# Two trunk layers on one core: features in four loads, an early activation, first products of one feature tile, and other numbers for the planner

## Chip, core and metric

The kernel runs on one core of a Trainium2 chip. The metric is the device time of one execution in microseconds (us), lower is better. Before the change three runs took 1011.51, 1011.09 and 1009.39 us; the median is 1011.09 us.

## What is computed

The reference is a two-layer backbone that serves 128 context tokens and 256 latent tokens with the same weights. Cut to what matters here, one layer is:

```python
m = silu(cvec) @ w_mod + b_mod                     # six vectors of 1024: shift, scale, gate, twice
h = rms(x, g_mix) * (1 + scale) + shift            # "modulated" features
cq, ckv, krope, na_q, na_k, na_v, df_q, df_k, df_v = split(h @ w_in)
o_mla, o_na, o_df = attention_A(...), attention_B(...), attention_C(...)
x = x + gate * (concat(o_mla, o_na, o_df) @ w_out)
h = rms(x, g_ffn) * (1 + scale2) + shift2
x = x + gate2 * ((silu(h @ w_gate) * (h @ w_up)) @ w_down)
```

All weights are float32. A float32 product is made as three matmuls of split halves: high x high, high x low, low x high (helper `mm3`, L357 to L359).

## The kernel before, in words

The features lie transposed in one tile `xT`, eight feature tiles (`KD = 8`) of 128 rows by 384 tokens. A layer has a planned part and a part in fixed order. The planned part holds everything from the modulation to the first output tiles: each step is a task with an engine, an assumed duration, the tasks it waits for, the buffers it takes, and a priority. The class `Plan` lays these tasks out in time with the assumed durations, tries 300 random changes of the priorities, and keeps the order that ends first in its own model. That order is then what each engine executes, strictly in sequence. So a changed duration in the plan can move any task of either layer. The FFN behind it has a fixed order.

The start of layer 0, where the changed lines stand, goes like this:

- **Loads.** SyncE issues `xT` in two halves (L260), then, in the plan's order, the modulation weights (`qu`, `ku` and `raw` from `w_mod`, L398) and the input weights (`raw` from `w_in`, L312). The small vector `cv` comes on ScalarE's queue.
- **Fillers.** TensorE begins with matmuls of `ones` with `ones` (L750) that compute nothing needed. Two numbers give how many (`WARMUP`): 18 at once and 16 pairs, which the plan may put wherever TensorE has nothing to do. One filler is two instructions in the profile.
- **Statistics.** ScalarE applies SiLU to `cv` (`sv`, L743), then squares the eight feature tiles (L759); VectorE adds them up (L763); TensorE sums over partitions (`t`, L771); GpSimd takes the power -1/2 (L522), VectorE makes a diagonal (L527), TensorE spreads it (L531), ScalarE copies it out (`bc`, L739).
- **Modulation.** Shift and scale come in four sets, each serving two feature tiles. A set is two steps of 16 matmuls (`m`, L408), one for each half of its weights, then a copy (L414), a transpose (L419), and the bias and scale on VectorE (L425, L454).
- **Modulated features.** For each feature tile: multiply by the norm (`nt`, L546), scale and shift (L554, on VectorE or GpSimd as `POOLK` says), high half (`hh`, ScalarE, L550), low half (`hl`, VectorE, L558).
- **First products.** The column chunks 0 and 1 of `w_in` are split into halves (`wh` on ScalarE, L285; `wl` on VectorE, L291) and multiplied with `hh` and `hl` for three token tiles each. A unit of the plan takes two feature tiles: six matmuls. With three token tiles, two chunks and four pairs this makes 24 units or, counted by single feature tiles, 48.

The attention of the layer follows, with more of `w_in` as dense work between its small matmuls.

## Time and profile before

| | before |
|---|---|
| median of three runs | 1011.09 us |
| the profiled execution | 1011.29 us |
| its span on the core | 1009.5 us |
| TensorE matmul busy | 995.5 us (99%) |
| VectorE busy | 721.8 us (71%) |
| ScalarE busy | 512.6 us (51%) |
| GpSimd busy | 174.4 us (17%) |
| first product (L357) starts | 22.87 us after the span's start |

Times of instructions are microseconds from the span's start. The busy share of TensorE includes the fillers and the overlap of pipelined matmuls, so a share of 99% doesn't say that 99% of the time is needed work. A row of the timeline gives start, length, engine, line, operation and tile; what stands in brackets is the idle time of that engine before it and what ended it. PE is TensorE's matmul, PEld its weight load, SPq SyncE's queue of DMA issues.

### The profile page before, as it was taken

How to read it: one execution, taken by the hardware profiler on the slowest of the kernel's cores; microseconds unless marked ns; L12 is line 12 of the kernel's file. 1: busy time of each engine (PE TensorE's matmuls, PEld its weight loads, DVE VectorE, ACT ScalarE, POOL GpSimd, SP SyncE). 2: the span in 40 equal slices, each digit the busy share in tenths (PEclk: the TensorE clock that was granted, in tenths of full speed). 3: DMA queues.
4: the chain of work that ended last, by engine and by line, in shares of the span. 5: the costliest groups of instructions: out<-in, count | busy, mean ns of one | idle time of the engine just before them, and what ended most of it. 6: DMA issues, size and time to landing. Idle time of an engine off the chain costs nothing.

```text
span 1009.5 us, 16623 instructions
## 1 busy us (share of the span) xinstructions
PE 995.5 (99%) x6074; PEld 929.6 (92%) x6074; DVE 721.8 (71%) x1637; ACT 512.6 (51%) x1206; POOL 174.4 (17%) x263
## 2 busy tenths in 40 slices
PE   9999999999999999999999999999999999999998
PEld 8877778899999999999978878888999999999998
DVE  4678778887999999964356887788889655554342
ACT  3466778765433333333326778796553433333221
POOL 2166123201000000100015633240010000000000
PEclk9999999999999999999999999999999999999999
DMA  9865643327575757684462143322574525244451
GB/s 361 329 200 180 193 135 125 108 87 255 186 242 186 240 181 225 188 278 136 126 216 96 48 152 90 106 89 82 195 243 148 165 88 163 85 127 123 131 146 37
DMA packets 128209, 163.82 MB, mean 162 GB/s; under 512 B 5120, under 2 KB 107136, under 8 KB 125824
## 3 DMA queue, kind: packets, MB, share of 16 engines
q1 hardware_dynamic: 119712, 134.33, 41.5%
q0 software_dynamic: 6832, 27.77, 7.9%
q8 instruction: 48, 0.79, 0.3%
q10 hardware_dynamic: 1584, 0.66, 0.2%
q14 instruction: 33, 0.27, 0.1%
HBM read 159.69 MB, written 3.05 MB: 161 GB/s over the span
## 4 chain that ended last, share of the span: by engine, by line
PE 89%; ACT 5%; DVE 2%; POOL 1%; DMA 1%; issue 1%; ACTq 0%; DVEq 0%; POOLq 0%
PE z L357 13%; PE z L359 13%; PE z L358 13%; PE t L358 6%; PE t L357 6%; PE t L359 6%; PE s L357 5%; PE s L358 5%; PE s L359 5%; PE s L1078 4%; PE t L1045 2%; PE m L408 2%; PE t L1181 1%; PE s L952 1%; PE s L750 1%
## 5 line engine op out<-in xcount | busy, mean ns | idle before, releaser
L285 ACT ACTIVATE wh<-raw 128x768 fp32r<-128x768 f32 (+3 forms) x224 | 203.5, 909 | 365.4 <-PE z L358 138.1
L291 DVE TENSOR_TENSOR wl<-raw,wh 128x768 fp32r<-128x768 f32 (+3 forms) x224 | 231.8, 1035 | 112.5 <-ACT wh L285 110.9
L357 PE MATMUL z<-fh,wh 128*128 128x386 f32 x304 | 103.2, 339 | 0.0
L358 PE MATMUL z<-fl,wh 128*128 128x386 f32 x304 | 103.1, 339 | 0.0
L357 PE MATMUL z<-wh,hh 128*128 128x384 f32 (+1 forms) x264 | 101.3, 384 | 1.8 <-ACT hh L550 1.4
L359 PE MATMUL z<-fh,wl 128*128 128x386 f32 x304 | 102.6, 338 | 0.0
L480 DVE CUSTOM_DVE_ANT_0 sums<-wt,sums,pcol 128x1024 f32<-128x1024 f32 x80 | 102.3, 1278 | 0.3 <-ACT sums L469 0.3
L359 PE MATMUL z<-wh,hl 128*128 128x384 f32 (+1 forms) x264 | 90.5, 343 | 0.5 <-DVE hl L558 0.5
L358 PE MATMUL z<-wl,hh 128*128 128x384 f32 (+1 forms) x264 | 90.0, 341 | 0.0
L578 POOL TENSOR_TENSOR small<-small,mhalf 128x4 f32<-128x4 f32 (+4 forms) x58 | 75.5, 1302 | 4.8
L357 PE MATMUL s<-fh,wh 128*128 128x386 f32 x200 | 68.2, 341 | 0.0
L357 PE MATMUL t<-fh,wh 128*128 128x386 f32 x200 | 68.1, 340 | 0.0
L358 PE MATMUL t<-fl,wh 128*128 128x386 f32 x200 | 67.8, 339 | 0.0
L358 PE MATMUL s<-fl,wh 128*128 128x386 f32 x200 | 67.7, 339 | 0.0
L359 PE MATMUL s<-fh,wl 128*128 128x386 f32 x200 | 67.5, 338 | 0.0
L359 PE MATMUL t<-fh,wl 128*128 128x386 f32 x200 | 67.5, 338 | 0.0
L1101 ACT ACTIVATE e<-s,small 128x384 f32<-128x384 f32 (+1 forms) x114 | 57.8, 513 | 15.2 <-DVE small L1090 9.0
L474 POOL DMA_DIRECT2D wt<-in_w_modT x40 | 21.5, 539 | 252.4 <-DVE mod L480 186.5
L357 PEld LDWEIGHTS z<-wh,hh 128*128 128x128 f32 x264 | 50.0, 189 | 11.0 <-issue 4.6
L358 PEld LDWEIGHTS z<-fl,wh 128*128 128x128 f32 x304 | 57.5, 189 | 0.0
L359 PEld LDWEIGHTS z<-fh,wl 128*128 128x128 f32 x304 | 57.3, 189 | 0.0
L357 PEld LDWEIGHTS z<-fh,wh 128*128 128x128 f32 x304 | 57.2, 188 | 0.0
(299 smaller groups left out, 2414.4 us busy)
## 6 DMA issues: line engine op xcount, KB each, us to landing
raw<-in_w_gate SPq DMA_DIRECT2D x22, 1024.0 KB, 6.2
raw<-in_w_up SPq DMA_DIRECT2D x22, 1024.0 KB, 5.4
raw<-in_w_down SPq DMA_DIRECT2D x32, 704.0 KB, 4.7
wt<-in_w_modT POOLq DMA_DIRECT2D x40, 512.0 KB, 4.1
raw<-in_w_mod SPq DMA_DIRECT2D x16, 1024.0 KB, 5.1
raw<-in_w_in SPq DMA_DIRECT2D x40, 384.0 KB, 4.0
raw<-in_w_out SPq DMA_DIRECT2D x8, 640.0 KB, 4.4
qu<-in_w_mod SPq DMA_DIRECT2D x8, 512.0 KB, 8.5
```

What stands on the lines that cost most here:

```text
L285: nc.scalar.activation(hi, src, AF.Copy)
L291: nc.vector.tensor_tensor(lo, src, hi.bitcast(F32), op=ALU.subtract)
L357: nc.tensor.matmul(out, sh, mh, start=first, stop=False)
L358: nc.tensor.matmul(out, sh, ml, start=False, stop=False)
L359: nc.tensor.matmul(out, sl, mh, start=False, stop=last)
L408: nc.tensor.matmul(self.pm[32 * g:32 * g + 32, :n], sv[:, kb + k, :], w[g // self.per][:, k, i * n:(i + 1) * n], start=(kb + k == 0), stop ...
L474: nc.gpsimd.dma_start(self.w[:, self.loaded % 3], w_modT[l, c * P:(c + 1) * P])
L480: nc.vector.tensor_tensor_reduce(self.junk, self.w[:, self.n % 3], self.s[:, v], 1.0, pcol[l][:, PC_BMOD + c:PC_BMOD + c + 1], ALU.mult, A ...
L578: nc.gpsimd.tensor_tensor(out, t[:, :n], mhalf[:, :n], op=ALU.pow)
L1045: nc.tensor.transpose(pt[:, b, :], x, ident)
L1078: nc.tensor.matmul(ps[:, i, :], q, k, start=True, stop=True)
L1101: nc.scalar.activation(x["e"][i], ps[:, j, :], AF.Exp, bias=x["mx"][:, i:i + 1], scale=-1.0 if bias else 1.0, accum_out=x["su"][:, i:i + 1])
```

## The change

- `xT` is loaded in four pieces of two feature tiles instead of two pieces of four; the squares wait for their own piece.
- An activation with SiLU on one column of `ones` is put right behind the issue of `cv`; its result is overwritten with the old constant.
- For the chunks 0 and 1 of layer 0 a unit of the first products takes one feature tile: three matmuls.
- The fillers become 24 at once and 40 single ones.
- One feature tile of layer 0 (tile 1) moves from GpSimd to VectorE for its scale and shift.
- The plan's assumed numbers change: the lag of a DMA 2.8 to 2.0, a modulation load 2.95 to 2.62, the first loads, the scale and shift 1.08/0.6 to 1.36/0.64. The lag and the last two hold for both layers.

The diff, cut to its core:

```diff
-POOLK = ((1, 3, 5, 7), (0, 2, 3, 4, 5, 6, 7))
+POOLK = ((3, 5, 7), (0, 2, 3, 4, 5, 6, 7))
-LAG = 2.8
+LAG = 2.0
-WARMUP = (18, 0.43, 16)
+WARMUP = (24, 0.215, 40)
-LOADX = 2.6
+LOADX = (2.3, 0.98)
...
     nc.scalar.dma_start(cv, cv_d)
+
+    nc.scalar.activation(mhalf[:, 15:16], ones[:, 0:1], AF.Silu)
+    nc.vector.memset(mhalf[:, 15:16], -0.5)
...
-    for k in range(0, KD, 4):
-        nc.sync.dma_start(xT[:, k:k + 4, :], xT_d[:, k:k + 4, :])
+    for k in range(0, KD, 2):
+        nc.sync.dma_start(xT[:, k:k + 2, :], xT_d[:, k:k + 2, :])
...
-            w = w0 = add(PE, WARMUP[1] / 2 * WARMUP[0], lambda *a: idle(WARMUP[0], *a), take=("s",), prio=URGENT)
+            w = w0 = add(PE, WARMUP[1] * WARMUP[0], lambda *a: idle(WARMUP[0], *a), take=("s",), prio=URGENT)
             for i in range(WARMUP[2]):
-                w = add(PE, WARMUP[1], lambda: idle(2), after=[w], prio=DENSE + 9)
+                w = add(PE, WARMUP[1], lambda: idle(1), after=[w], prio=DENSE + 9)
             add(DVE, 0.0, lambda: None, after=[w], frees=[w0])
-            sums, loaded = [], [add(DMA, LOADX, lambda: None, prio=0.0) for _ in range(2)]
+            add(DMA, LOADX[0], lambda: None, prio=4 * URGENT)
+            sums, loaded = [], [add(DMA, LOADX[1], lambda: None, prio=2 * URGENT) for i in range(4)]
...
-                sums.append(add(ACT, 0.42, square, after=[loaded[k // 4]], take=("row",), prio=k))
+                sums.append(add(ACT, 0.42, square, after=[loaded[k // 2]], take=("row",), prio=k))
...
-                    ld = add(DMA, 2.95, lambda *kind, ms=ms, kb=kb: ms.load(kb, *kind), take=("un|raw",), prio=PPRIO[part])
+                    ld = add(DMA, 2.62, lambda *kind, ms=ms, kb=kb: ms.load(kb, *kind), take=("un|raw",), prio=PPRIO[part])
...
-            b = add(POOL if on_pool else DVE, 1.08 if on_pool else 0.6, lambda k=k, x=x, e=nc.gpsimd if on_pool else nc.vector: norm_aff(l, k, x["t"], e),
+            b = add(POOL if on_pool else DVE, 1.36 if on_pool else 0.64, lambda k=k, x=x, e=nc.gpsimd if on_pool else nc.vector: norm_aff(l, k, x["t"], e),
...
-                    u = add(PE, 6 * (n / 2400 + 0.0135), unit, after=[lo, last[t], hready[kb], hready[kb + 1]],
-                            take=((kind[t] if len(kind) > 1 else kind),) if kb == 0 else (), frees=[hi], prio=DENSE)
+                    for k in ((0,), (1,)) if l == 0 and ci < 2 else ((0, 1),):
+                        def unit(*tag, t=t, kb=kb, w=w, ks=k):
...
+                        u = add(PE, 3 * len(k) * (n / 2400 + 0.0135), unit, after=[lo, last[t]] + [hready[kb + i] for i in k],
+                                take=((kind[t] if len(kind) > 1 else kind),) if first else (), frees=[hi], prio=DENSE)
```

What the plan makes of it stands in the order of the instructions. The changed file is longer, so a line of before has a number that is 3 lower at this place (L750 is L753 after). First TensorE, from the kernel's start to its first product, before: `s` is the fillers' bank, `t` the sum and the spread of the statistics and the transpose, `m` a modulation set, whose two halves of weights are told apart by the number of `qu`, and `z` the first product. Rows that only repeat are left out.

```order
L750 MATMUL s_137<-ones 128x128 x34
L408 MATMUL m_206<-qu_157,sv 32x128 x2
L771 MATMUL t_223<-ones,sq_163 128x1 x3
L750 MATMUL s_137<-ones 128x128 x6
L408 MATMUL m_206<-qu_176,sv 32x128 x2
L531 MATMUL t_265<-dg_259,ones 128x384
L750 MATMUL s_137<-ones 128x128 x4
L419 MATMUL t_283<-ident,mev_269 128x128
L750 MATMUL s_137<-ones 128x128 x6
L408 MATMUL m_303<-qu_235,sv 32x128 x2
L408 MATMUL m_303<-qu_275,sv 32x128 x2
L357 MATMUL z_359<-wh_263,hh_119 128x416
```

The same stretch after the change, and the first step of the second set (`m_351`) behind the first product.

```order
L753 MATMUL s_141<-ones 128x128 x26
L775 MATMUL t_200<-ones,sq_169 128x1 x3
L411 MATMUL m_204<-qu_171,sv 32x128 x2
L753 MATMUL s_141<-ones 128x128 x6
L534 MATMUL t_239<-dg_231,ones 128x384
L753 MATMUL s_141<-ones 128x128 x9
L411 MATMUL m_204<-qu_221,sv 32x128 x2
L753 MATMUL s_141<-ones 128x128 x6
L422 MATMUL t_302<-ident,mev_289 128x128
L753 MATMUL s_141<-ones 128x128 x17
L360 MATMUL z_339<-wh_284,hh_123 128x416
L411 MATMUL m_351<-qu_298,sv 32x128 x2
```

Four steps of `m` stand ahead of the first product before, two after; 50 fillers become 64, and of those behind the sum of the squares 16 become 38. The second half of the first set now stands behind the spread and nine fillers; it stood ahead of the spread.

SyncE's loads at the start, before (`qu_157` and `qu_176` with their `ku` are the two halves of the first modulation set, `qu_235` begins the second):

```order
L260 DMA xT<-in_xT 128x1536 x2
L398 DMA qu_157<-in_w_mod 128x1024
L398 DMA ku_158<-in_w_mod 128x1024
L398 DMA qu_176<-in_w_mod 128x1024
L398 DMA ku_177<-in_w_mod 128x1024
L312 DMA raw_204<-in_w_in 128x832
L312 DMA raw_227<-in_w_in 128x768
L398 DMA qu_235<-in_w_mod 128x1024
```

And after. Here `qu_171` and `qu_221` are the halves of the first set; `qu_192` and `ku_193` between them belong to the third set, whose matmuls come behind the second's.

```order
L263 DMA xT<-in_xT 128x768 x4
L401 DMA qu_171<-in_w_mod 128x1024
L401 DMA ku_172<-in_w_mod 128x1024
L401 DMA qu_192<-in_w_mod 128x1024
L401 DMA ku_193<-in_w_mod 128x1024
L401 DMA qu_221<-in_w_mod 128x1024
L401 DMA ku_222<-in_w_mod 128x1024
L315 DMA raw_241<-in_w_in 128x832
L315 DMA raw_249<-in_w_in 128x768
L401 DMA qu_261<-in_w_mod 128x1024
```

The second half of the first set has moved two transfers of 512 KB back.

VectorE from the first set's scale to the first low halves, before:

```order
L454 SCALAR_TENSOR_TENSOR aff_103<-mod_101,pcol_105 128x4
L554 TENSOR_SCALAR nt_287<-nt_287,aff_103,mod_101 128x256
L554 TENSOR_SCALAR nt_287<-nt_287,aff_103,mod_101 128x128
L291 TENSOR_TENSOR wl_300<-raw_227,wh_281 128x768
L558 TENSOR_TENSOR hl_120<-nt_287,hh_119 128x384
```

And after, where the scale and shift of the second feature tile (`nt_259`) stands on VectorE too, ahead of the first low half:

```order
L457 SCALAR_TENSOR_TENSOR aff_107<-mod_105,pcol_109 128x4
L557 TENSOR_SCALAR nt_251<-nt_251,aff_107,mod_105 128x256
L557 TENSOR_SCALAR nt_251<-nt_251,aff_107,mod_105 128x128
L557 TENSOR_SCALAR nt_259<-nt_259,aff_107,mod_105 128x256
L557 TENSOR_SCALAR nt_259<-nt_259,aff_107,mod_105 128x128
L294 TENSOR_TENSOR wl_324<-raw_249,wh_295 128x768
L561 TENSOR_TENSOR hl_124<-nt_251,hh_123 128x384
```

Behind the start the plans of both layers are reshuffled as well. Counted over TensorE's whole order: from the end of the 48 first products to the FFN of layer 0 the dense products (L357 to L359) are resumed after other work 44 times before and 57 times after; in layer 1's planned part 63 times before and 66 after. The rows of the FFN stand as they were, but for the places where they meet the planned part.

More of the change, by code (lines that the diff above doesn't have):

```diff
@@ L819, in weights @@
                 if pairs:
-                    lead = add(DMA, 2.95 / 4096 * n, lambda: w_raw(rk, src, rs, 0), take=("raw", "graw"), prio=pairs[0])
-                    lead.mate = add(DMA, 2.95 / 4096 * n, lambda: w_raw(rk, src, rs, 1), after=[lead], prio=pairs[1])
+                    lead = add(DMA, 2.62 / 4096 * n, lambda: w_raw(rk, src, rs, 0), take=("raw", "graw"), prio=pairs[0])
+                    lead.mate = add(DMA, 2.62 / 4096 * n, lambda: w_raw(rk, src, rs, 1), after=[lead], prio=pairs[1])
                 else:
@@ L840, in g1 @@
                 for t in range(3):
-                    def unit(*tag, t=t, kb=kb, w=w):
-                        if tag:
-                            z[t] = acc(tag[0])
-                        s = slice(t * P, (t + 1) * P)
-                        for k in range(2):
-                            mm3(z[t][:, :n], hh[:, kb + k, s], hl[:, kb + k, s], w["h"][:, k, :], w["l"][:, k, :],
-                                kb + k == 0, kb + k == KD - 1)
-                    u = add(PE, 6 * (n / 2400 + 0.0135), unit, after=[lo, last[t], hready[kb], hready[kb + 1]],
-                            take=((kind[t] if len(kind) > 1 else kind),) if kb == 0 else (), frees=[hi], prio=DENSE)
-                    u.dense = 1
-                    plan.dense += 1
-                    last[t] = u
-                    if kb == 0:
-                        room[t] = u
+                    for k in ((0,), (1,)) if l == 0 and ci < 2 else ((0, 1),):
+                        def unit(*tag, t=t, kb=kb, w=w, ks=k):
+                            if tag:
+                                z[t] = acc(tag[0])
+                            s = slice(t * P, (t + 1) * P)
+                            for k in ks:
+                                mm3(z[t][:, :n], hh[:, kb + k, s], hl[:, kb + k, s], w["h"][:, k, :], w["l"][:, k, :],
+                                    kb + k == 0, kb + k == KD - 1)
+                        first = kb + k[0] == 0
+                        u = add(PE, 3 * len(k) * (n / 2400 + 0.0135), unit, after=[lo, last[t]] + [hready[kb + i] for i in k],
+                                take=((kind[t] if len(kind) > 1 else kind),) if first else (), frees=[hi], prio=DENSE)
+                        u.dense = 1
+                        plan.dense += 1
+                        last[t] = u
+                        if first:
+                            room[t] = u
                     if kb == KD - 2 and done:
```

## The prediction

> **What bounds the kernel now.** I read the page first, then busy time by stage, then the timeline of the first 60 us. The page names TensorE:
>
> ```profile
> span 1009.5 us, 16623 instructions
> PE 995.5 (99%) x6074; PEld 929.6 (92%) x6074; DVE 721.8 (71%) x1637; ACT 512.6 (51%) x1206; POOL 174.4 (17%) x263
> ```
>
> The profiled execution took 1011.29 us, so 1.8 us lie outside its span; it is 0.2 us above the median of 1011.09. All sums below are made against 1011.29. What a measurement here can tell from no change is about 0.2%, that is 2 us.
>
> The stages, with the columns stretch, length, then TensorE's busy time and count first (rows of the stages from the first products on; the last of the three is layer 1's planned part):
>
> ```profile
> 22.87:57.43 34.56, 34.52 (x294) 30.31 (x292) 21.31 (x76) 18.63 (x52) 7.91 (x17) 1.00 0.87 324
> 57.43:206.00 148.57, 145.75 (x948) 116.56 (x948) 119.93 (x341) 112.05 (x355) 57.94 (x81) 1.00 0.46 148
> 525.84:706.00 180.16, 175.91 (x1061) 152.35 (x1062) 143.63 (x390) 132.14 (x413) 72.63 (x103) 0.99 0.32 100
> ```
>
> From the first product at 22.87 to the end of the 48 units at 57.43 TensorE idles 0.04 us. In the middle of layer 0 it idles 148.57 - 145.75 = 2.8 us, in layer 1's planned part 4.25 us. So TensorE's needed work is a fixed sum, and the end moves by what TensorE spends on other things: fillers and waits before 22.87, waits behind it, and the cost of changing between kinds of matmul. The start, where the change is aimed:
>
> ```profile
> 1.05 10.64 PE L750 MATMUL s<-ones 128*128 128x128 f32 x68 [1.05 <-DVE ones L251]
> 5.30 1.28 ACT L743 ACT_TABLE_LOAD   x1 [5.30 <-DMA cv<-in_cv]
> 6.71 3.74 ACT L759 ACTIVATE sq<-xT 128x384 f32<-128x384 f32 x8
> 8.08 4.47 DVE L763 TENSOR_TENSOR sq<-sq,sq 128x384 f32<-128x384 f32 x7 [6.79 <-ACT sq L759]
> 12.63 0.83 PE L771 MATMUL t<-ones,sq 128*128 128x1 f32 x6
> 13.29 1.42 PEld L750 LDWEIGHTS s<-ones 128*128 128x128 f32 x12
> 14.52 0.90 ACT L285 ACTIVATE wh<-raw 128x832 fp32r<-128x832 f32 x1 [4.06 <-DMA raw<-in_w_in]
> 14.83 0.11 PEld L408 LDWEIGHTS m<-qu,sv 128*32 128x32 f32 x2
> 15.84 0.30 PEld L531 LDWEIGHTS t<-dg,ones 128*128 128x128 f32 x2 [0.20 <-issue]
> 17.37 0.14 PEld L419 LDWEIGHTS t<-ident,mev 128*128 128x128 f32 x1
> 17.80 0.36 DVE L425 TENSOR_TENSOR mod<-t,pcol 128x2 f32<-128x2 f32 x4
> 18.39 0.67 DVE L554 TENSOR_SCALAR nt<-nt,aff,mod 128x256 f32<-128x256 f32 x2
> 18.97 0.95 DVE L291 TENSOR_TENSOR wl<-raw,wh 128x768 fp32r<-128x768 f32 x1
> 19.02 0.14 PEld L408 LDWEIGHTS m<-qu,sv 128*32 128x32 f32 x4
> 19.84 0.55 DVE L558 TENSOR_TENSOR hl<-nt,hh 128x384 fp32r<-128x384 f32 x1
> 21.87 0.30 PE L408 MATMUL m<-ku,sv 128*32 128x128 f32 x2 [0.87 <-DMA ku<-in_w_mod]
> 22.87 0.46 PE L357 MATMUL z<-wh,hh 128*128 128x416 f32 x1
> ```
>
> The reader is to see that the first product waits for nobody: its first low half begins at 19.84, but TensorE's order puts the second modulation set ahead, and that waited for its load until 21.87. Before 22.87 TensorE has done all four steps of the first two sets.
>
> **The early activation and the four loads.** The table load of 1.28 us stands between `cv` (5.30) and the squares. Moved to the start it costs ScalarE nothing, since it had nothing to do before 5.30. SiLU of `cv` still stands ahead of the squares and still waits for 5.30. From the end of the table load to the first square it was 6.71 - 6.58 = 0.13 us, so the squares begin at 5.43, one each 3.74 / 8 = 0.47 us.
>
> The Trainium skill, page "ScalarE: Activation LUTs", section "What ACT_TABLE_LOAD costs", gives 1283 ns for the load and about 1380 ns of drain, 2.66 us for a switch; by it the squares would begin another 1.4 us sooner. This trace has the 1.28 us and the square 0.13 us behind it, no drain, so the measurement decides.
>
> Do the features come in time? The last half lands late:
>
> ```profile
> 0.73 0.85 SPq L260 DMA_DIRECT2D xT<-in_xT  x2
> DMA to landing us min/median/max: 4.3/5.3/6.4
> ```
>
> The second half is issued near 1.2 and lands near 7.5; four pieces of the same bytes end at about the same time, and the seventh square isn't due before 5.43 + 6 x 0.47 = 8.2. The first quarter lands no later than the first half did, at about 0.7 + 4.3 = 5.0. Four loads are issued in place of two, 0.4 us each, so the loads behind them go out 0.8 us later, hidden by the queue of bytes.
>
> The additions: before, the first one waited for the third square (8.08), now it needs two: 5.43 + 0.94 = 6.36. The seven and the wait behind them took 12.63 - 8.08 = 4.55 us, so the sum over partitions starts at 10.9 instead of 12.63. That is 1.7 us won, and the question is where it goes.
>
> **From the sum to the first product.** TensorE's order fixes this. I need the price of a filler:
>
> ```profile
> 5.00:6.00 1.00, 1.00 (x7) 1.00 (x6) 1.00 0.98 408
> 9.00:10.00 1.00, 1.00 (x12) 1.00 (x11) 1.00 1.02 410
> ```
>
> The counts of instructions in one microsecond, 7 and then 12, show that the first fillers run at about half speed; the step lies near 7.3. With the 68 instructions of 10.64 us that makes (estimate) 0.22 us for one at first and 0.11 later; a filler is two, so 0.22 us. The first 26 fillers end near 9.9. Behind the sum, from the rows above: sum 13.29 - 12.63 = 0.66; a step of `m` 15.84 - 14.83 = 1.01; six fillers 14.83 - 13.29 = 1.54; spread and nine fillers (17.37 - 15.84) + 5 x 0.22 = 2.63; a step 1.01; six fillers 1.54; transpose and 17 fillers (19.02 - 17.37) + 11 x 0.22 = 4.07. Together 12.46 us. The first product starts at 10.9 + 12.5 = 23.4, 0.5 later than before, and nothing can bring it below the sum's start + 12.5.
>
> Does anything bind more than the fillers? The second half of the first set is now behind 1.05 MB more. Before, the `raw` of 0.43 MB behind it landed at 14.52, so it had landed itself near 13.4. At the rate of this row (slices of 1.5 us)
>
> ```profile
> GB/s 0 177 398 411 383 377 396 309 416 423 404 418 415 401 399 407 412 399 409 408 396 385 376 399 374 374 407 442 398 280 360 40 0 53 373 251 280 294 115 203
> ```
>
> 1.05 MB are 2.6 us, so near 16.0; TensorE gets there at 10.9 + 0.66 + 1.01 + 1.54 + 2.63 = 16.75. VectorE: transpose at 19.3, bias 0.43 later, low half 2.04 after that as before (17.80 to 19.84) plus the other tile's 0.58 (18.39 to 18.97): 22.4 to 22.9, the second tile's to 23.4. Without the fillers the product could start 0.9 us earlier at best.
>
> **What the products must now carry.** Of the first four steps of `m` two come behind the first product. What a step costs there:
>
> ```profile
> 28.94 0.33 PE L359 MATMUL s<-wh,hl 128*128 128x384 f32 x1
> 29.21 0.30 PE L408 MATMUL m<-qu,sv 128*32 128x128 f32 x2
> 30.22 0.44 PE L357 MATMUL t<-wh,hh 128*128 128x384 f32 x1
> 30.50 0.33 PE L358 MATMUL t<-wl,hh 128*128 128x384 f32 x1
> 23.74 0.46 PE L357 MATMUL z<-wh,hh 128*128 128x416 f32 x1
> 24.63 0.36 PE L357 MATMUL z<-wh,hh 128*128 128x416 f32 x1
> ```
>
> From 28.94 to 30.50 are 1.56 us; two products at their pace would be 0.35, so a single step costs 1.21 and a pair in a row 2.22. Before: four single, 4.84. After: two pairs and two single, 6.86. That is +2.0. Back come the waits of the first two tiles: 22.87 to 23.74 and to 24.63 are 0.87 and 0.89 us for three matmuls that take 0.57, so -0.6, since in the new order the halves are there by 23.4. The rest of the stretch stays bound by TensorE: loads are the same bytes, and the closest call, tile 2's low half behind the parameters on VectorE, comes at about the time TensorE gets there. Start in all: 0.5 + 2.0 - 0.6 = +1.9 us. Splitting the units buys little here: the first unit of one tile starts when both tiles are nearly ready. Tile 1's move to VectorE is in the sum (0.58), under the fillers.
>
> **The reshuffled middle.** The order shows 13 more resumptions of dense products in layer 0 and 3 more in layer 1. One costs
>
> ```profile
> 103.96 0.42 PE L357 MATMUL z<-wh,hh 128*128 128x384 f32 x1
> 104.22 0.34 PE L358 MATMUL z<-wl,hh 128*128 128x384 f32 x1
> 110.24 0.34 PE L357 MATMUL z<-wh,hh 128*128 128x384 f32 x1
> 110.41 0.34 PE L358 MATMUL z<-wl,hh 128*128 128x384 f32 x1
> ```
>
> 0.26 against 0.17 us: 0.09 behind transposes, nothing behind scores. Sixteen are 0 to 1.4; I take 1.0, as most stand behind transposes. The waits of the middle (2.8 and 4.25 us) are drawn anew by the new plan. I count them at no change; they can fall by 7 at most, and could as well rise by as much.
>
> **Sum.** 1011.29 + 1.9 + 1.0 = 1014.2 us, 0.3% slower.
>
> **Rivals.**
> - *The middle gives it back.* The plan now assumes loads nearer to this trace, so its order may avoid waits such as
>
> ```profile
> PE s L1078 <- ACT e L1101: 1.0, 1, 1.0
> ```
>
>   If half of the 7.07 us goes: 1014.2 - 3.5 = 1010.7, no change. If three quarters go: 1014.2 - 5.3 = 1008.9, faster; that decides from 5.1 us on. For it speaks that both plans are new; against it, that these waits hang on chains of ScalarE and VectorE behind the same products, which no edited line shortens. Chances 0.18 and 0.13.
> - *New waits in the middle*, half as many again: +3.5, 1017.7. The old middle has few waits, and 16 more changes of kind speak for it. Chance 0.12.
> - *The clock drops.* Between the first fillers (9.9) and the sum (10.9) TensorE idles 1.0 us. If it fell to half speed, the six fillers would take 1.3 longer and the spread 0.3: 1015.8. Against it: between the layers it idled almost as long and the next step kept its pace of 1 us for eight:
>
> ```profile
> 519.27 0.83 PE L513 MATMUL s<-ones,sq 128*128 128x1 f32 x6 [0.83 <-ACT sq L492]
> 520.03 1.92 PE L408 MATMUL m<-early,sv 128*32 128x512 f32 x16
> ```
>
>   The Trainium skill, page "TensorE: Matmul & The Clock Gate", section "Part 1: The HAM clock gate", has the clock at half until a window of about 3.4 us was busy and again after an idle window of that length; by that rule 1.0 us is too short. The trace agrees in the first half (slow to about 7.3). Chance 0.10.
>
> That the early activation doesn't do what it says (a second table load at `cv`) would cost back 1.3 us, 1015.5; it lies in the range and gets no chance of its own.
>
> **How the numbers follow.** The forecast has 0.47, its own range 1012.4 to 1016.0 (`cv` landing 1 us earlier, or the resumptions and a wait twice as dear). Slower by over 0.2% (above 1013.1): 0.42 of the forecast, 0.12 and 0.10, so 0.64. Within 0.2%: 0.05 of the forecast and 0.17 of the half, so 0.22. Faster (below 1009.1): 0.14. The range for 8 in 10 runs from 1008.9, which leaves out the better half of the faster case, to 1018.0, which leaves out the worse half of the new waits.
>
> **What would show it.** Right: no table load behind `cv`; squares near 5.4; the sum near 10.9; 17 fillers up to the first product near 23.4; the 48 units ending 2 to 3 us later for equal work. Wrong: a first product before 22, idle time of TensorE in the two middles well below 7 us, or the second half of the first set waited for.

## The result, and the profile after

The change made the kernel slower, and by far more than forecast: 1022.51 us (median of four runs, 1021.47 to 1024.58) against 1011.30 us before in the same comparison. The ratio is 1.0111, with a 95% interval of 1.0092 to 1.0130. Forecast were 1014.2 us in a range of 1008.9 to 1018.0. The sign was right, the range was not.

The page's first lines after the change:

```profile
span 1021.4 us, 16687 instructions
PE 1002.8 (98%) x6102; PEld 933.2 (91%) x6102; DVE 721.1 (71%) x1640; ACT 510.9 (50%) x1207; POOL 169.3 (17%) x261
```

The span grew by 11.9 us. TensorE's busy time grew by 7.3 us, though the kernel's needed work is the same; the other 4.6 us are idle time of TensorE. To see where, both spans are cut at equal work: the first product, the 120th product of layer 0's FFN, the sum of the squares behind layer 0, the 120th FFN product of layer 1. Busy time by stage, before (columns as in the stages of the prediction; the second value is the length, the third TensorE's busy time):

```profile
22.87:258.53 235.66, 232.80 (x1548) 198.21 (x1547) 182.47 (x507) 159.76 (x457) 71.02 (x105) 1.00 0.54 181
258.53:517.70 259.17, 259.17 (x1473) 258.09 (x1473) 203.71 (x377) 96.74 (x147) 16.90 (x32) 1.00 0.62 197
517.70:747.89 230.19, 224.83 (x1357) 196.77 (x1356) 180.60 (x469) 157.70 (x454) 79.25 (x112) 0.99 0.39 125
```

And after:

```profile
24.19:268.46 244.27, 237.28 (x1614) 201.50 (x1612) 182.33 (x509) 159.36 (x459) 69.17 (x103) 0.99 0.52 173
268.46:527.60 259.14, 259.14 (x1473) 258.06 (x1473) 204.32 (x376) 95.22 (x143) 17.42 (x33) 1.00 0.62 199
527.60:760.32 232.72, 226.90 (x1359) 195.59 (x1358) 179.24 (x469) 157.46 (x455) 77.26 (x112) 0.99 0.39 124
```

Up to the first product the change lost 24.19 - 22.87 = 1.3 us. From there to FFN product 120 it lost 8.6. In the rest of layer 0's FFN it lost nothing, in layer 1 2.5, of which 0.5 comes back behind it (261.08 against 261.61 us). That makes 11.9. So almost three quarters of the loss lie between the first product and FFN product 120, where the forecast had put some 2.2 us (2.0 for the steps of `m`, -0.6 for the first waits, and layer 0's 13 of the 16 resumptions that it priced at 1.0 us).

Reading that stretch row by row gives four places.

**1. The start.** ScalarE first, then TensorE's clock:

```profile
1.17 1.28 ACT L257 ACT_TABLE_LOAD   x1 [1.17 <-PEq L1790]
4.56 2.82 ACT L763 ACTIVATE sq<-xT 128x384 f32<-128x384 f32 x6
8.17 0.94 ACT L763 ACTIVATE sq<-xT 128x384 f32<-128x384 f32 x2 [0.79 <-DMA xT<-in_xT]
```

```profile
8.00:9.10 1.10, 1.10 (x10) 0.92 (x9) 0.62 (x2) 0.93 (x2) 0.00 (x0) 1.00 0.97 317
9.10:10.30 1.20, 0.01 (x1) 0.00 (x0) 1.12 (x2) 0.01 (x1) 0.00 (x0) 1.00 1.01 413
10.30:12.10 1.80, 1.76 (x38) 1.56 (x38) 0.16 (x1) 0.00 (x0) 0.64 (x1) 1.00 1.01 396
12.10:14.80 2.70, 2.70 (x16) 2.69 (x13) 0.68 (x3) 0.00 (x0) 0.23 (x1) 0.50 1.05 425
14.80:15.80 1.00, 1.00 (x4) 0.58 (x3) 0.00 (x0) 0.00 (x0) 0.00 (x0) 0.65 0.98 392
```

The early activation did what it says: its table load ran at 1.17, beside nothing else, and the squares began at 4.56. The sum over partitions began at 10.34. But TensorE had nothing from 9.1 to 10.3, then only the sum (its matmuls move one column) and a step of `m` (its weights are 32 columns wide, two of them filled, where a filler has 128), and from 12.1 on its granted clock (the third value from the end) was 0.50. I call these two narrow matmuls. The six fillers and the spread took 15.8 - 12.1 = 3.7 us; in before the same took 1.54 + 0.75 = 2.3 (the spread from 15.84 to the next filler at 16.59). That is the clock rival, 1.4 us; the forecast had priced it at 1.6.

**2. Steps of `m` behind the first product.** Busy time of their line alone, before and after, from the first product to FFN product 120:

```profile
22.87:258.53 235.66, 17.20 (x258) 6.18 (x256) 1.00 0.54 181
```

```profile
24.19:268.46 244.27, 19.77 (x320) 8.28 (x320) 0.99 0.52 173
```

Two more steps stand there (320 instructions for 258 in the rows, 32 to a step), 2.6 us. The forecast had 2.0.

**3. Waits for modulation weights behind the first product**, which before didn't have. Two of the waiting steps, and from the chain of waits the loads they waited for (start, then length):

```profile
56.42 1.06 PE L411 MATMUL m<-raw,sv 128*32 128x512 f32 x8 [0.64 <-DMA raw<-in_w_mod]
73.14 1.07 PE L411 MATMUL m<-raw,sv 128*32 128x512 f32 x8 [1.33 <-DMA raw<-in_w_mod]
```

```profile
48.97 7.40 DMA raw<-in_w_mod
65.81 7.28 DMA raw<-in_w_mod
```

With a third wait of 0.28 at 35.45 that is 2.25 us. A load took over 7 us from issue to landing, and the new order left it less. By the profile's chain the first was issued when a step of `m` (47.91 to 48.95) had ended, the second behind a store in SyncE's queue (L907) that had waited for GpSimd until 63.92.

**4. The hand-over to the FFN.** When the attention is done, each layer loads a vector of 1 MB (`sums`, L470) into a buffer that comes free with the last product of the output projection, and ScalarE applies SiLU to it (L472). ScalarE, GpSimd and TensorE there, after:

```profile
243.74 0.54 POOL L470 DMA_DIRECT2D sums<-in_crow  x1
253.00 1.28 ACT L472 ACT_TABLE_LOAD   x1 [7.91 <-DMA sums<-in_crow]
254.29 1.91 ACT L472 ACTIVATE sums<-sums 128x2048 f32<-128x2048 f32 x1
256.11 2.94 ACT L288 ACTIVATE wh<-raw 128x1024 fp32r<-128x1024 f32 x3
257.20 0.44 PE L360 MATMUL z<-fh,wh 128*128 128x386 f32 x1 [1.62 <-ACT wh L288]
258.15 0.69 PE L360 MATMUL t<-fh,wh 128*128 128x386 f32 x1 [0.33 <-ACT wh L288]
```

```profile
258.00:261.20 3.20, 3.05 (x7) 2.44 (x8) 3.20 (x6) 1.53 (x3) 0.45 (x1) 0.50 0.26 33
```

ScalarE stood 7.91 us in front of `sums`, with three splits of FFN weights queued behind it. TensorE ran out of split weights, waited 1.62 and 0.33 us, and then its clock was 0.50 for 3.2 us. Instruction by instruction the FFN's products lost 3.6 us here, and the spread among them 0.35. In layer 1 ScalarE waited 7.3 us at the same place; the products lost 0.69 + 0.33 us of waiting and about 1.0 between instructions. In all some 6 us in this execution, about half of it waiting and half the clock and gaps between instructions. Before, ScalarE had two splits ahead of the same wait:

```profile
243.80 2.01 ACT L285 ACTIVATE wh<-raw 128x1024 fp32r<-128x1024 f32 x2 [6.02 <-PE z L358]
245.82 1.28 ACT L469 ACT_TABLE_LOAD   x1
247.12 1.92 ACT L469 ACTIVATE sums<-sums 128x2048 f32<-128x2048 f32 x1
```

They kept ScalarE until 245.82, and by then `sums` had practically landed. The load itself took as long before as after: 8.5 to 8.7 us from issue to landing, 8.6 to 9.2 after.

So the ledger of the 11.9 us between these two executions is: 1.3 to the first product (of which the clock took 1.4 and the earlier sum gave some back), 2.6 for the steps of `m`, 2.25 for their loads, 4.0 for the hand-over of layer 0, 2.0 for that of layer 1; what is left, -0.3, is the rest of the middle. The order of the planned part decides places 2 and 3, and place 4 hangs on where one instruction stands in ScalarE's order. My theory after the result was that these are mostly losses of the particular order that the plan drew, not of the edits. The rival was that the edits, above all the lag of 2.0 us, bring them about.

### The profile page after: what moved, and what is told of

It reads as the page before. It is cut to its first block, busy times and chain, and to the rows that moved or that the text cites. A ratio compares the mean times of both kernels' runs of the same rounds, so it can differ in the third digit from the quotient of the medians.

```text
span 1021.4 us, 16687 instructions
## 1 busy us (share of the span) xinstructions
PE 1002.8 (98%) x6102; PEld 933.2 (91%) x6102; DVE 721.1 (71%) x1640; ACT 510.9 (50%) x1207; POOL 169.3 (17%) x261
## 4 chain that ended last, share of the span: by engine, by line
PE 84%; ACT 4%; DVE 4%; DMA 3%; POOL 2%; issue 2%; SPq 0%; ACTq 0%; DVEq 0%; POOLq 0%
PE z L360 12%; PE z L361 12%; PE z L362 12%; PE t L360 6%; PE t L361 6%; PE t L362 6%; PE s L361 5%; PE s L360 5%; PE s L362 5%; PE s L1084 3%; PE t L1051 2%; PE m L411 2%; PE t L1187 2%; POOL small L581 2%; DMA raw<-in_w_mod 1%
## 5 line engine op out<-in xcount | busy, mean ns | idle before, releaser
L581 POOL TENSOR_TENSOR small<-small,mhalf 128x4 f32<-128x4 f32 (+4 forms) x58 | 73.2, 1262 | 4.8
```

The costliest lines, as they stand in the source:

```text
L581: nc.gpsimd.tensor_tensor(out, t[:, :n], mhalf[:, :n], op=ALU.pow)
```

## The experiments

Each was timed against before in the same comparison, so ratios are compared, not medians.

| kernel | median us | ratio to before | 95% interval |
|---|---|---|---|
| after | 1022.51 | 1.0111 | 1.0092 to 1.0130 |
| after_silu_late | 1018.45 | 1.0082 | 1.0061 to 1.0104 |
| after_fill_gap | 1020.78 | 1.0109 | 1.0092 to 1.0126 |
| after_silu_late_fill5 | 1019.58 | 1.0089 | 1.0070 to 1.0108 |
| after_lag28 | 1013.84 | 1.0037 | 1.0025 to 1.0049 |
| after_lag28_set1 | 1014.72 | 1.0037 | 1.0023 to 1.0051 |
| after_draw1 | 1014.54 | 1.0029 | 1.0019 to 1.0039 |
| after_draw2 | 1013.43 | 1.0025 | 1.0015 to 1.0036 |
| after_draw4 | 1012.85 | 1.0016 | 1.0006 to 1.0026 |
| before_silu_late | 1010.09 | 1.0000 | 0.9991 to 1.0009 |
| before_act_four | 1010.74 | 0.9998 | 0.9989 to 1.0008 |
| before_lag20 | 1015.30 | 1.0045 | 1.0032 to 1.0059 |
| before_draw1 | 1012.73 | 1.0020 | 1.0010 to 1.0029 |
| before_draw10 | 1016.59 | 1.0056 | 1.0040 to 1.0071 |
| before_layer1_draw1 | 1008.98 | 0.9977 | 0.9968 to 0.9986 |

**The hand-over alone: after_silu_late and before_silu_late.** The SiLU of `sums` gets a bias of zero that is made from the row norms' copy, so it can't stand ahead of that. The order of the planned part stays word for word; in the FFN behind it some instructions change places.

```diff
-            nc.scalar.activation(self.s, self.s, AF.Silu)
...
+        def silu(self, rb):
+            zero = small(1)
+            nc.vector.tensor_scalar(zero, rb[:, 0:1], 0.0, None, op0=ALU.mult)
+            nc.scalar.activation(self.s, self.s, AF.Silu, bias=zero)
...
                 nc.scalar.activation(rb, next(rstd), AF.Copy)
+                sums.silu(rb)
```

> After, with the SiLU of the broadcast vector at the start of each FFN (sums, L472) made to wait for the copy of the row norms (rb), so that ScalarE splits the next weights before it; nothing is left out. Theory (the hand-over): in the changed kernel ScalarE waited 7.9 us in layer 0 and about 7 us in layer 1 for the load of sums, the splits of the FFN weights queued behind it, and TensorE lost 1.62 + 0.33 us of waiting and about 1.7 + 0.3 us of slow clock in layer 0, 0.69 + 0.33 and about 1.0 us in layer 1: 6.0 us in all. Without that the time is 1022.5 - 6.0 = 1016.5 us, and no wait of TensorE for wh over 0.5 us is left at the hand-overs. Rival (the FFN weights come late anyway, because their buffers come free late): the wait for wh only changes its name and the time stays within 1 us of 1022.5.

> Before, with the same edit as after_silu_late; nothing is left out. Theory (the hand-over of before loses nothing, since ScalarE reached sums only when it had landed): within 1 us of before, 1010 to 1012 us. Rival (the edit is a gain in itself, whatever the plan): 3 to 6 us faster than before.

Before stayed where it was (1.0000), so the edit is no gain in itself. After came out 0.3% lower by the ratios, about 2.9 us and not 6, and the intervals overlap, so the times alone don't show the gain. The trace shows the theory's step and where part of the gain went. No wait for `wh` is left among TensorE's waits (place, releaser, total us, times, longest):

```profile
PE m L411 <- DMA raw<-in_w_mod: 1.8, 3, 1.1
PE m L411 <- DMA ku<-in_w_mod: 1.6, 1, 1.6
PE m L411 <- DMA qu<-in_w_mod: 0.9, 1, 0.9
```

Against before's trace the FFN's products up to the 120th in layer 0 now cost 0.05 us more, where after had 3.6, and in layer 1 0.1, where after had 2.0; that wait is undone. But the waits for modulation weights are 4.3 us in this execution, at the same order, where the profiled execution of after had 2.25, and the granted clock was 0.93 and 0.90 in the two stretches of 10 us from 30 to 50. So place 3 varies from one execution to the next. The six executions of this kernel lie between 1016.0 and 1022.8 us.

**The clock alone: after_fill_gap.** The planned order is after's but for the first row on TensorE.

```diff
-... lambda *a: idle(WARMUP[0], *a), take=("s",), prio=URGENT)
+... lambda *a: idle(WARMUP[0] + 11, *a), take=("s",), prio=URGENT)
```

> After, with 37 fillers in place of 26 ahead of the sum of the squares, the order otherwise the same; only needless work is added. Theory (the clock falls because TensorE is nearly idle from 9.1 to 12.1 us: 1.2 us of waiting and then matmuls with one or two columns): the eleven fillers of 0.11 us fill the wait, the clock stays at 1.00 from 12.1 to 15.8, the six fillers take 1.5 us in place of 2.7, the spread 0.8 in place of 1.0; the first product starts near 22.7 in place of 24.2, and the time is 1022.5 - 1.4 = 1021.1 us. Rival (small matmuls don't count as work, so that the sum and the step of m alone let the clock fall): the granted clock is 0.5 for some 3 us again and the first product stays near 24.2.

The stretch by stage:

```profile
8.00:11.20 3.20, 3.20 (x31) 3.20 (x30) 1.70 (x4) 0.94 (x2) 0.00 (x0) 1.00 0.99 361
11.20:12.90 1.70, 1.70 (x40) 1.49 (x39) 0.16 (x1) 0.00 (x0) 0.65 (x1) 1.00 1.00 395
12.90:14.30 1.40, 1.40 (x16) 1.40 (x13) 0.68 (x3) 0.00 (x0) 0.22 (x1) 1.00 1.03 421
```

With the gap filled the clock stays at 1.00, and the six fillers take 1.4 us, though the sum and the step of `m` still stand there for 1.7 us. So here the sum and the step of `m` alone, 1.7 us, didn't let the clock fall, against what the rival says. It is one execution, and the last section shows that the place of the quiet stretch counts as well as its length. The time was not won: I had taken a filler for 0.11 us, but it is two instructions, 0.22 us. Eleven of them ran until 11.2, put the sum 0.9 us later, and the first product came at 24.05. The waits for modulation weights were 4.1 us behind it.

This trace also says what the hand-over costs without a drop of the clock. ScalarE's order there is after's, with no split ahead of `sums`, yet TensorE waited less in layer 0 and its clock stayed at 1.00:

```profile
256.69 0.44 PE L360 MATMUL z<-fh,wh 128*128 128x386 f32 x1 [0.43 <-ACT wh L288]
```

Against before's trace the products and the spread cost 1.3 us more in layer 0 and the products 1.8 in layer 1, together 3.2 where after's execution had 6.0. So the 6 us are the price in one execution, and removing the hand-over need not be worth as much in others. At a mean granted clock of 1.00, two runs of after_silu_late took 1016.0 and 1016.7 us, three of after_fill_gap 1019.9 to 1020.1. That difference of 3.2 to 4.1 us agrees with 3.2, though the two kernels differ in their fillers too.

**The lag, forward and back: after_lag28 and before_lag20.**

```diff
-LAG = 2.0
+LAG = 2.8
```

> After, with the plan's assumed lag of a load back at 2.8 us; nothing else, though the plan draws a new order from it. Theory (the plan puts steps of the modulation 0.8 us too early because it expects their loads 0.8 us too soon): TensorE's waits for the modulation weights behind the first product (0.28 + 0.64 + 1.33 us in after) fall below 0.5 in all, and the time falls by about 2 us, if the redrawn middle and the hand-overs stay as they are; these can move it by 4 us either way. Rival (the loads are late because of the bytes ahead of them): waits of over 1.5 us for the modulation weights remain.

> Before, with the plan's assumed lag of a load at 2.0 us in place of 2.8; nothing else of the change, and a new order drawn from it. In its order two splits of FFN weights stand on ScalarE between the last square and sums at both hand-overs, as in before; in after none stands there. Theory (the shorter lag makes the plan put steps of the modulation before their loads have landed; the loss at the hand-over is a second effect that hangs on that place in the order): TensorE waits 1.5 us or more for modulation weights behind the first product (before: none), no wait over 0.5 for wh at the hand-overs, time 1010.1 + 2 to 4 = 1012 to 1014 us. Rival 1 (the lag is the whole loss): 1016 us or more. Rival 2 (the lag hurts only with the new order of the first loads): waits for modulation weights under 0.8 us, 1009 to 1011.5.

after_lag28 lost only 0.37% to before; the forecast's sum was 0.29%. Its waits for modulation weights were 0.8 us behind the first product and 0.3 ahead of it, and at layer 0's hand-over one split stands ahead of `sums` and keeps ScalarE busy:

```profile
248.15 1.06 ACT L288 ACTIVATE wh<-raw 128x1024 fp32r<-128x1024 f32 x1 [6.69 <-PE z L361]
249.22 1.28 ACT L472 ACT_TABLE_LOAD   x1
```

That looked like the lag being the cause. before_lag20 goes against it: with the short lag and nothing else of the change it lost 0.45%, more than the theory's 0.2 to 0.4%, but only one wait for modulation weights behind the first product came up (1.0 us at 76.24). Its dearest wait is another, in layer 1, between scores and a weight load:

```profile
538.16 2.29 PE L995 MATMUL s<-ku,ckT 128*128 128x384 f32 x4 [2.22 <-issue]
```

So the lag doesn't bring the 2.25 us of waits by itself. A new number means a new order, and each order has its own waits.

**Redraws: after_draw1, after_draw2, after_draw4, before_draw1, before_draw10.** The only edit is the start of the generator that the 300 trials are drawn from; here for start 1:

```diff
-        draw = random.Random(0)
+        draw = random.Random(1)
```

> After, with another start for the random numbers from which the plan's 300 trials are drawn; nothing else. In its order two splits of FFN weights stand between the last square and sums at both hand-overs, as in before. Theory (the 6 us of the hand-over hang on that place, which a redraw moves, and not on the edited lines): no wait over 0.5 us for wh at the hand-overs, 1022.5 - 6 = 1016.5 us, give or take 3 for the redrawn middle; the waits for modulation weights (lag 2.0) stay at 1.5 us or more. Rival (the loss is in the edits, whatever is drawn): 1020 us or more.

> After, with start 2 for the random numbers of the plan; nothing else. Its order has two splits of FFN weights ahead of sums at both hand-overs. Theory (the changed kernel's order was an unlucky draw; other draws end as after_draw1 did): no wait over 0.5 us for wh at the hand-overs, 1012 to 1017 us. Rival (after_draw1 was the exception): 1019 us or more.

> After, with start 4 for the random numbers of the plan; nothing else. Its order has two splits of FFN weights ahead of sums at both hand-overs. Theory, as for after_draw2: 1012 to 1017 us, no wait over 0.5 us for wh at the hand-overs; together with after_draw1 and after_draw2 it shows how far a redraw alone moves the time. Rival: 1019 us or more.

> Before, with start 1 for the random numbers of the plan; nothing else. Its order has two splits of FFN weights ahead of sums at both hand-overs, as before. Theory (a redraw alone moves the time by some microseconds, and the order of before was a lucky one): 1011 to 1015 us. Rival (redraws of before all end near 1010; only the edits cost): 1009 to 1011 us.

> Before, with another start (10) for the random numbers of the plan's 300 trials; nothing else. Of the redraws of before whose order was looked at, this is one where no split of FFN weights stands on ScalarE between the last square and sums at layer 0's hand-over, as in after; at layer 1's two stand there. Theory (that place in the order makes the hand-over's loss, with or without the change): TensorE waits over 1 us for wh at layer 0's hand-over and its clock falls behind that, 3 to 4 us lost there, none at layer 1's. Rival (the loss needs the edits of the change): no wait over 0.5 us for wh. The time: 1010.1 + 3.5 and the redrawn middle, 1012 to 1018 us.

With all edits and a lag of 2.0 us, three other draws ended 0.29, 0.25 and 0.16% over before. None waits for `wh` at a hand-over, and their waits for modulation weights behind the first product are 0, 0.2 and 0 us (after_draw1 and after_draw2 have one of 0.5 and 0.8 ahead of it). My expectation for after_draw1 that 1.5 us of these would stay failed with that: they are not a matter of the lag alone. The loss at the start is no mark of after's order either: in after_draw1 the clock was 0.50 from 13.35 to 16.76 us. By stage, FFN product 120 of layer 0 came 2.3 to 5.4 us later in the three than in before, and layer 1 up to the same point took 1.3 to 3.4 us less than in before's trace, of which some 1.5 us are a drop of the clock in that trace (layer 1 is 1.5 us shorter in those of before_act_four and before_silu_late, in the same order). before_draw1 lost 0.20% by a redraw alone; its first product came at 26.99, 4.1 us later than in before, and what it got back lies in layer 1, 3.8 us shorter than in before's trace.

before_draw10 has none of the change's edits, but in layer 0 no split ahead of `sums`:

```profile
248.03 1.28 ACT L469 ACT_TABLE_LOAD   x1 [7.71 <-DMA sums<-in_crow]
251.14 2.94 ACT L285 ACTIVATE wh<-raw 128x1024 fp32r<-128x1024 f32 x3
252.24 0.44 PE L357 MATMUL z<-fh,wh 128*128 128x386 f32 x1 [0.83 <-ACT wh L285]
```

ScalarE waited 7.71 us, and TensorE 0.83 + 0.34 for `wh` and 0.35 for `wl`. That shows that the place in the order makes the wait, without the change. The price was 2.3 us and not 3 to 4, since the clock stayed at 1.00 this time; the first part of the expectation (over 1 us) holds only for the sum of two waits. In the changed kernel's orders from the starts 1 to 12, two splits stand ahead of `sums` at both hand-overs for nine, as in before; for the starts 3, 6 and 11 none stands there at one of the two. None at both, as in after, comes from none of these, so after's own order is a rare one in this respect.

**The edits of the code alone: before_act_four.** The early activation and the four loads in before, with before's plan:

```diff
+    nc.scalar.activation(mhalf[:, 15:16], ones[:, 0:1], AF.Silu)
+    nc.vector.memset(mhalf[:, 15:16], -0.5)
...
-    for k in range(0, KD, 4):
-        nc.sync.dma_start(xT[:, k:k + 4, :], xT_d[:, k:k + 4, :])
+    for k in range(0, KD, 2):
+        nc.sync.dma_start(xT[:, k:k + 2, :], xT_d[:, k:k + 2, :])
```

> Before, with only the early activation and the features in four loads; the plan, and so the order of every engine but for these instructions, is as before. Theory (TensorE's order and the load of the second modulation set fix the first product, not the squares): the squares start near 4.6 and the sum of the squares is ready 1 us or more sooner, yet the first product stays at 22.8 +- 0.3 and the time at 1010.1 +- 1. Rival (the squares bound the start): the first product near 21.5, the time 1008.8 us.

```profile
8.68 0.94 ACT L762 ACTIVATE sq<-xT 128x384 f32<-128x384 f32 x2 [0.97 <-DMA xT<-in_xT]
12.69 0.83 PE L774 MATMUL t<-ones,sq 128*128 128x1 f32 x6
23.40 0.46 PE L360 MATMUL z<-wh,hh 128*128 128x416 f32 x1
```

The last two squares, which now wait 0.97 us for their piece of the features, are done at 9.62, yet the sum starts at 12.69, with no wait in its row: TensorE's fillers and its first step of `m` stand ahead of it. The first product is 0.3 us above the upper bound that I gave, the squares began at 5.12 and not near 4.6, and the time is unchanged (0.9998). These two edits are worth nothing that can be measured by themselves; what costs or gains is the order.

**The first set's loads first: after_lag28_set1.**

```diff
-..., take=("un|raw",), prio=PPRIO[part])
+..., take=("un|raw",), prio=PPRIO[part] if part else 2 * URGENT)
```

> After, with the lag back at 2.8 us and the loads of the first modulation set ahead of all other weights; nothing is left out. In its order both steps of the first set stand ahead of the sum of the squares again, and one step of the second set ahead of the first product. Theory (in the changed kernel the first product waits for the chain from the second half of the first set, which landed behind 1 MB of other weights): the first product comes at 18 to 21 us in place of 24, TensorE loses part of it again to waits for the second set (1 to 3 us), and the time is 1013.8 - 2 = 1012 us, 1010 to 1013.5. Rival (the loads are the bound of the first 45 us, whose sum doesn't change): an earlier first product is given back in full, 1013 to 1016 us.

```profile
9.91 0.41 PE L411 MATMUL m<-qu,sv 128*32 128x128 f32 x4 [1.56 <-DMA qu<-in_w_mod]
12.67 4.41 PE L753 MATMUL s<-ones 128*128 128x128 f32 x28
18.03 0.83 PE L775 MATMUL t<-ones,sq 128*128 128x1 f32 x6
```

This failed. The plan put both steps of the first set and 14 fillers ahead of the sum, the first step waited 1.56 + 0.77 us for its load, the clock fell, and the sum began only at 18.03. The first product came at 26.48. An instruction that waits for a load holds up everything behind it on its engine, here the sum of the squares. The time equals after_lag28's (both 1.0037), so the time is in the rival's range, but no earlier first product was there to be given back: neither side of my expectation had the way it went.

**Two losses out at once: after_silu_late_fill5.** The edit of after_silu_late, and 5 more fillers in place of 11.

> After, with the two losses that the traces price taken out together: the SiLU of sums behind the copy of the row norms, as in after_silu_late, and 5 more fillers (10 matmuls, 1.1 us) ahead of the sum of the squares; the order is otherwise after's. Theory (the losses add): the hand-overs give back 6.0 us and the clock 1.4 us, so 1022.5 - 7.4 = 1015.1 us if the waits for modulation weights stay at the 2.2 us of after, up to 1017.2 if they are 4.3 as in after_silu_late; the granted clock stays at 1.00 from 9 to 17 us. Rival (the losses hide each other): no faster than after_silu_late, 1018.5.

The clock was 1.00 from 8 to 17 us, the first product came at 23.63, and no wait for `wh` is left; but 1.0089 is no better than after_silu_late, and my sum of the losses is missed by 2.4 to 4.5 us. Its 6.0 us for the hand-over were the price in one execution, as after_fill_gap's trace shows. In this execution the waits for modulation weights are 2.1 + 2.0 us (0.6 of them ahead of the first product), and the steps of `m` behind the first product take 20.04 us, where each of the three redraws has 18.21, with one step fewer there. So after's order keeps a loss of 3 to 4 us in the waits for these loads, which the two edits don't touch. Why it isn't 1015 us in every execution stays open: the profiled one took 1017.9 us, the others up to 1023.1. The runs of after's order with these edits scatter by 4.9 to 6.8 us (after's own four by 3.1), those of the other orders in the table by 2.2 to 3.6.

**A version below both: before_layer1_draw1.** The layers draw apart, layer 0 from start 0 and layer 1 from start 1.

```diff
-        draw = random.Random(0)
+        draw = random.Random(Plan.drawn)
+        Plan.drawn += 1
```

> Before, with start 0 for the random numbers in layer 0, as it was, and start 1 in layer 1; nothing else. Theory (the layers' draws can be chosen apart; layer 1 of before_draw1 was 2.2 us shorter than in the other traces of before's own order): 1011.3 - 2.2 = 1009.1 us, a version under both kernels. Rival (layer 1's order depends on what layer 0 leaves, and the gain isn't there): 1010.5 to 1013.

Its part from the sum behind layer 0 to the end, against before's:

```profile
519.53:1006.20 486.67, 480.73 (x2813) 452.42 (x2813) 321.10 (x723) 247.44 (x585) 76.66 (x116) 1.00 0.40 127
```

```profile
519.27:1009.50 490.23, 482.05 (x2813) 453.75 (x2813) 323.74 (x723) 246.56 (x585) 81.37 (x116) 1.00 0.40 126
```

It is 3.6 us shorter than in before's profiled execution (in which the granted clock was 0.83 from 530 to 540 us) and 1.9 shorter than in that of before_act_four, whose order there is before's (488.55). The time is 0.23% below before, with an interval of 0.9968 to 0.9986, without any of the change's edits.

## Why the prediction was wrong, step by step

- **The early activation and the four loads: right.** No table load behind `cv`; squares at 4.56 (5.43 forecast, since `cv` landed 0.8 us earlier here); the last piece of the features was waited for 0.79 us, which I had excluded: it landed near 8.17 and not 7.5. The sum came at 10.34 in place of 10.9.
- **From the sum to the first product: right in its parts but for the clock.** 13.85 us against 12.46. The difference of 1.4 is the six fillers and the stretch of the spread at half clock. The order did set the first product: 24.19 in place of 23.4, with the 17 fillers up to it as forecast.
- **The clock rival was set aside with the wrong row.** I compared the gap of 1.0 us with one of 0.83 us between the layers, behind which steps of `m` with 512 columns follow. Here a wait of 1.23 us was followed by 1.8 us of narrow matmuls. It was 1.23 and not 1.0 although the sum came earlier, since the 26 fillers ended at 9.11 and not 9.9: their pace doubled near 5.3 us, where I had taken before's 7.3. after_fill_gap had no such wait and no drop; after_draw4 has nearly the same wait, 1.19, but fillers behind the sum, and no drop.
- **The moved steps of `m`: right, the term too small,** 2.6 us against 2.0. The sign that I had named, 48 units ending 2 to 3 us later, failed: the 144th of the products with `hh` and `hl` (48 units of three) ended near 62.4 in place of 57.4, 5.0 us later. The start (1.3), the steps of `m` (2.6) and two of the waits (0.9) make 4.8 of it.
- **"The waits of the middle ... I count them at no change": this step failed first.** In this order 2.25 us of waits for modulation weights came in, up to 4.3 in the executions of the edited versions of it. The rest of the middle was near the forecast: layer 0 kept the sum of its other waits within 0.2 us.
- **The hand-over to the FFN had no term at all: this cost most, 6 us in the profiled execution and 3.2 in after_fill_gap's, where the clock held.** The rows of the middle that the forecast rests on end at 206.00 us, ahead of it. The text said that the FFN's rows stand as they were but for the places where they meet the planned part, and those places got no price. The program's order is fixed, but where it meets the plan the instructions of an engine are placed anew, and ScalarE's wait for `sums` moved ahead of the splits. Its place could have been read before the run: `sums` takes 8.5 us from issue to landing in before's trace, its issue hangs on the last product of the output projection, and ScalarE's order after the change showed nothing between the last square and that wait.
- **The range treated the rivals as exclusive.** New waits, the clock and the hand-over came together. The rival "new waits" alone (1017.7) and the clock (1015.8) would have made 1019 with the forecast's sum, outside the range I gave.
- **The forecast's sum fits the other orders.** The same edits with four other orders (three redraws and the old lag) ended 0.16 to 0.37% over before; 1014.2 was 0.29% over. That doesn't show that its terms were right. In the three redraws FFN product 120 of layer 0 came 2.3 to 5.4 us later, where they say 2.7, and layer 1 came between 1.8 us shorter and 0.3 longer than in before_act_four's trace, where they say 0.2 longer. Before's own redraws, without any edit, ended 0.20 and 0.56% over before. So the agreement may be luck. What was missing is the spread between orders: the new orders of both layers without after's hand-over lie between 0.16 and 0.45% over before, edits or not. That before's own order is better than all of these suggests that a new draw was more likely to lose than to gain; before_layer1_draw1, which keeps its layer 0, shows that one can gain.

What stays open: how the loss that remains without the hand-over and the drop of the clock divides, why the waits for the modulation loads, which take over 7 us in this order, vary between executions, and what places the SiLU of `sums` where it stands in ScalarE's order; only its effect was shown.

## What to carry to other kernels

Where numbers of a planner are changed, price the redraw itself: its own scatter, taken from a few redraws of the kernel before, belongs into the range, and a new order has no reason to be as good as one that was kept. Read the new order at the seams between planned and unplanned parts, engine by engine: ScalarE's wait for a slow load cost TensorE nothing behind two splits, and 1.3 to 4.0 us ahead of them. And a transfer or an operation that comes earlier gains nothing where the order of the waiting engine, filled with needless work, fixes the time, as before_act_four showed.

## What the runs showed of the hardware

A short wait can halve TensorE's clock when little work follows it. The clock changed in steps that lie on a grid. In each of the 16 traces a stretch at half clock inside the span lasts 3.41 us, if there is one, and in after all changes lie whole multiples of 3.41 us apart: full clock from 5.26, half from 12.09 (2 of them later), 257.84 (74) and 530.91 (154). Where the grid lies differs between executions: the first change to full clock came 3.3 to 6.0 us after the first filler. Up to that change fillers' instructions start 0.21 us apart, behind it 0.11; the clock column has no entry before it and reads 1.00 there.

Slices of this grid in after, two from the start and the one ahead of the drop at the hand-over:

```profile
8.67:12.09 3.42, 2.19 (x42) 1.81 (x41) 1.33 (x4) 0.43 (x2) 0.63 (x1) 1.00 1.01 401
12.09:15.50 3.41, 3.41 (x18) 3.08 (x15) 0.68 (x3) 0.00 (x0) 0.24 (x1) 0.50 1.03 417
254.43:257.84 3.41, 1.77 (x9) 1.12 (x7) 1.60 (x4) 3.41 (x3) 0.00 (x0) 1.00 0.01 2
```

In the slice from 8.67 to 12.09 TensorE ran 0.44 us of fillers, idled 1.23 us and then had only narrow matmuls; in the next slice the clock was half. At the hand-over 1.77 us of FFN products in a slice weren't enough either. A wait across the border of two slices had no such effect: after_draw4's of 1.19 us, from 9.19 to 10.38, left 2.8 us of busy time in each, and the clock held.

```profile
6.35:9.76 3.41, 2.84 (x25) 2.65 (x24) 2.79 (x5) 1.97 (x6) 0.00 (x0) 1.00 1.01 366
9.76:13.18 3.42, 2.80 (x42) 2.69 (x46) 2.09 (x6) 0.86 (x1) 0.87 (x1) 1.00 0.98 362
```

Busy time alone doesn't decide. In before_lag20 the clock held behind the first of these slices, in after_draw1 it fell behind the second, which has almost the same busy time, with 0.83 us of the sum in it against 0.30:

```profile
9.72:13.14 3.42, 2.37 (x43) 1.84 (x41) 2.64 (x5) 0.90 (x2) 0.00 (x0) 1.00 1.02 384
9.93:13.35 3.42, 2.32 (x38) 1.93 (x40) 1.39 (x5) 0.00 (x0) 0.87 (x1) 1.00 1.03 422
```

How much of what work keeps the clock up isn't shown. The Trainium skill, page "TensorE: Matmul & The Clock Gate", section "Part 1: The HAM clock gate", has the clock fall after an idle window of about 3.4 us that runs freely, without regard to the kernel. The slices of 3.41 us and their changing place agree with such a window; that the window must be idle doesn't, since TensorE was idle for only 1.23 us of it in after.

So the same program has executions with and without a drop, and their times differ. Of the twelve runs of before_layer1_draw1, five with a mean granted clock of 0.999 or 1.000 took 1007.6 to 1008.0 us, the seven with 0.997 or 0.998 took 1008.8 to 1009.8.
